# Three more groups of projections by one level of Strassen's method, with their late products moved into the next units

## The chip, the cores and the metric

One core of a Trainium2 chip runs the kernel, in float32 throughout. The metric is the device time of one execution in microseconds (us). About 0.2% is what a measurement of this kernel can tell from no change.

## What is computed

A layer of a streaming encoder on x (512 positions x 1024 channels):

```python
h = rmsnorm(x, norm_mix_g)
u, v, bg, cg, xs, ga, gb = split(h @ w_in)            # seven projections 1024 -> 1024
a = gelu(u) * (W_s[g] (block causal) rmsnorm(gelu(v)) + b_s[g])           # branch A
c = bg * causal_dwconv3(cg * xs, conv_w)                                  # branch B
m = sigmoid(ga + b) * (a @ w_proj_a) + sigmoid(gb + b) * (c @ w_proj_b)
x = x + m @ w_out
x = x + relu(rmsnorm(x, norm_ff_g) @ w_ff1)**2 @ w_ff2                    # 1024 -> 4096 -> 1024
y = rmsnorm(x, norm_final_g)
```

## The kernel before

Activations lie transposed: a tile is 128 channels by the 512 positions. Every float32 operand of TensorE is split in two, hi (a cast on ScalarE, ACT, L95) and lo (the difference, on VectorE, DVE, L96), and a product is three matmuls: hi by hi, hi by lo, lo by hi.

**A unit** is one output tile of a projection: 8 slices of the contraction x 3 = 24 matmuls of 128x512 (`unit_matmuls`, L189 to L191) with one operand of 128x1024 hi and lo. **A pair** is two output tiles of FF1 at once by one level of Strassen's method: the positions are halved, the contraction is halved, and seven products of 4 slices x 3 matmuls of 128x256 (`product`, L493 to L495; 84 matmuls) replace two units' 48. It uses combinations of the weights (three operands of 128x1024 and one of 128x512, sums on DVE in `plan_pairs`, L460, L466, L467) and of the activations (`combos`), and joins the products on DVE and ACT (`block_pair`, L514 to L529). Its seventh product P7 runs inside the next pair.

Order of the work: v, then u with the mixing of branch A behind it by LAG units (`mix`), gate A and P_A in turns, branch B (`c_units`: c, x and b of one tile in turns), gate B and P_B in turns, W_o, and four chunks of FF1 pairs and FF2 units. Only FF1 goes by pairs. A list of steps (`steps`) prepares the weights in that order: `pump` does the next step before a unit or product, when one of RING = 4 hi/lo buffers is free. A step records an ACT cast and a DVE subtraction, so both engines' queues mix the weights' work with that of the outputs. Weights come from HBM on SP's queue, 1 MB at a time into two raw buffers; the next but one is loaded when a raw buffer's last step has run. x is kept in `res` from the start to the residual of W_o. Storage is in groups by name (X, V, M, AC). The vector of per-channel constants (`vec`) comes on GpSimd's queue; the norm gain of x is a 513th column of x.

The engines' queues are in program order as the tile framework's scheduler set them.

Of the kernel before, what the change touches and what calls it, by code (L numbers as in the profile page):

```python
# [17 lines left out]
KT = D // P  # L18
NB = S // P
HALF = 512  # L20
# [6 lines left out]
RING = 4  # L27


V_BGATE, V_GV, V_CONV, V_GFF, V_GFIN, V_N = 0, 16, 24, 48, 56, 64  # L30
# [3 lines left out]
def hybrid_block(ctx, tc, xT, vecs, w_v, w_main, w_ff1, w_s, b_s, out_a, out_b):  # L34
# [16 lines left out]
    wsp = ctx.enter_context(tc.tile_pool(name="wsp", bufs=RING))  # L51
# [7 lines left out]
    nc.gpsimd.dma_start(vec, vecs)  # L59
# [17 lines left out]
    def shared(tag, bufs, name, dtype=F32):  # L77

        return big.tile([P, S], dtype, tag=tag, bufs=bufs, name=name)

    def wide(tag, name, dtype=F32, shape=(2, S)):

        return big.tile([P, *shape], dtype, tag=tag, bufs=4 if tag == "V" else 8, name=name)
# [18 lines left out]


# [3 lines left out]
    n_units = w_main.shape[0]  # L107
    steps = []
    opnds = []
    raw_of = {}  # L110

    def load(key):
        if key in raw_of:
            return
        r = raws.tile([P, 4, S], F32, name="raw")
        kind, i = key
        if kind == "u":
            nc.sync.dma_start(
                r.rearrange("p (u a) s -> p u (a s)", u=2), w_main[i : i + 2].rearrange("u p f -> p u f")
            )  # L120
        else:
            nc.sync.dma_start(r, w_ff1[i])
        raw_of[key] = r

    loads = []

    def load_after(key):

        n = loads.index(key) + 2
        if n < len(loads):  # L130
            load(loads[n])

    def add_operand(src, n=2, last=None):

        o = {"done": False, "ready": False, "idx": len(opnds)}

        def step():
            hi = wsp.tile([P, n, S], F32R, name="whi", padded_shape=[P, 2, S])
            lo = wsp.tile([P, n, S], F32R, name="wlo", padded_shape=[P, 2, S])
            split_into(hi, lo, src())  # L140
            o["hi"], o["lo"], o["ready"] = hi, lo, True
            if last:
                load_after(last)

        opnds.append(o)
        steps.append((step, o))
        return o

    def pump(n=1):

        while steps and n:
            step, o = steps[0]
            if o is not None and o["idx"] >= RING and not opnds[o["idx"] - RING]["done"]:
                return
            steps.pop(0)
            step()
            n -= 1
# [5 lines left out]
    units = []  # L163

    def plan_units(n):
        for _ in range(n // 2):
            i = len(units)
            key = ("u", i)
            loads.append(key)
            for e in range(2):  # L170
                units.append(add_operand(
                    lambda key=key, e=e: raw_of[key][:, 2 * e : 2 * e + 2, :], last=key if e else None
                ))
# [3 lines left out]
    def unit_matmuls(psum, act_hi, act_lo, start=True, stop=True, cols=slice(0, S), ks=range(KT), o=None):  # L177

        if o is None:
            o = units[state["next"]]  # L180
            state["next"] += 1
            pump()
            need(o)
            o["done"] = True
        hi, lo = (o[h].rearrange("p a s -> p (a s)") for h in ("hi", "lo"))
        for k in ks:
            c = slice(k * P, (k + 1) * P)
            first, end = start and k == 0, stop and k == KT - 1
            nc.tensor.matmul(psum, hi[:, c], act_hi[k][:, cols], start=first, stop=False)  # L189
            nc.tensor.matmul(psum, hi[:, c], act_lo[k][:, cols], start=False, stop=False)  # L190
            nc.tensor.matmul(psum, lo[:, c], act_hi[k][:, cols], start=False, stop=end)  # L191

    def bank():
        return ps.tile([P, S], F32, name="bank")
# [28 lines left out]


    resg = [big.tile([P, S + 1], F32, name=f"res{k}") for k in range(KT)]
    res = [t[:, :S] for t in resg]

    def halves_of(tag, name, dtype=F32R, n=KT):

        ts = [wide(tag, f"{name}{k}", dtype) for k in range(n)]  # L230
        return [t[:, 0, :] for t in ts], [t[:, 1, :] for t in ts]

    xh, xl = halves_of("X", "x")
    acc = shared("acc", 1, "acc")
    vtt = halves_of("V", "vt", F32, NB)
    vt = [[vtt[h][b] for h in range(2)] for b in range(NB)]
    wsT = wide("M", "wsT", F32, (KT, P))
    bsb = wide("M", "bsb", F32, (KT, P))
    vsum = small.tile([P, 2, NB], F32, name="vsum")

    vparts = {}
    vraw = []
    n_plain = n_units - NCH * KT
    plan_units(n_plain)

    def prep_v(i):
# [4 lines left out]
        if h == 0:  # L251
            nc.sync.dma_start(resg[k], xT[k])
        if i % 2 == 0:
            vraw.append(wide("AC", f"vraw{i}"))
        t = vraw[-1][:, i % 2, :]
        nc.sync.dma_start(t, w_v[h, k])
        if i == 2 * KT - 1:
            for key in loads[:2]:
                load(key)
        vp = wide("M", f"vp{h}{k}", F32R)  # L260
        vh, vl = vp[:, 0, :], vp[:, 1, :]
        if h == 0:
            split_into(xh[k], xl[k], res[k], scale=resg[k][:, S : S + 1])
        split_into(vh, vl, t)
        if h == 0:
            sum_squares(acc, res[k], k)
        vparts[i] = (vh, vl)

    def sum_squares(acc, src, k, n=S):
        if k == 0:  # L270
            nc.scalar.activation(acc, src, AF.Square)
        else:
            sq = temp("sq", n)
            nc.scalar.activation(sq, src, AF.Square)
            nc.vector.tensor_add(acc, acc, sq)
# [11 lines left out]
    V_AHEAD = 3  # L287
# [4 lines left out]
    for i in range(2 * KT):  # L292
# [6 lines left out]
        vh, vl = vparts.pop(i)  # L299
        for ws, xs in ((vh, xh), (vl, xh), (vh, xl)):  # L300
            for b in range(NB):
# [3 lines left out]
                )  # L305
        if i == KT - 1:
# [16 lines left out]
    nc.vector.tensor_copy(R, Rp)
    R2 = shared("R2", 1, "R2")
# [11 lines left out]
    ah, al = halves_of("AC", "a")  # L336
    us = {}

    def u_unit(j):
# [4 lines left out]
        u = temp("u")  # L344
        nc.scalar.activation(u, t, AF.Gelu)
        us[j] = u

    def mix(g):
# [11 lines left out]
        a = temp("a")  # L360
        nc.vector.tensor_mul(a, t, us.pop(g))
        split_into(ah[g], al[g], a)

    def c_units(j):
        pc = bank()
        unit_matmuls(pc, xh, xl)
        t = temp("t_c")
        nc.vector.tensor_mul(t, pc, R2)
        px = bank()
        unit_matmuls(px, xh, xl)  # L370
        z = temp("z", S + 2)
        nc.vector.memset(z[:, 0:2], 0.0)
        nc.vector.tensor_mul(z[:, 2 : S + 2], t, px)
        y = temp("y")
        w = [col(V_CONV + 8 * i, j) for i in range(3)]
        nc.vector.tensor_scalar(y, z[:, 0:S], w[0], None, op0=ALU.mult)
        for i in (1, 2):
            nc.vector.scalar_tensor_tensor(y, z[:, i : S + i], w[i], y, op0=ALU.mult, op1=ALU.add)
        pb = bank()
        unit_matmuls(pb, xh, xl)  # L380
        yr = temp("yr")
        nc.vector.tensor_mul(yr, y, R)
        c = temp("c")
        nc.vector.tensor_mul(c, pb, yr)
        split_into(ch[j], cl[j], c)

    def gate(n, j):
        pg = bank()
        unit_matmuls(pg, xh, xl)
        t = temp("t_g")  # L390
        nc.vector.tensor_mul(t, pg, R)
        sg = temp("sig")
        nc.scalar.activation(sg, t, AF.Sigmoid, bias=col(V_BGATE + 8 * n, j))
        return sg

    LAG = 2
    for j in range(KT):
        u_unit(j)
        if j >= LAG:
            mix(j - LAG)  # L400


    m1p = halves_of("V", "m1", F32, KT // 2)
    m1 = [m1p[k % 2][k // 2] for k in range(KT)]
    for j in range(KT):
        sg = gate(0, j)
        if j == 0:
            for g in range(KT - LAG, KT):
                mix(g)
        pp = bank()  # L410
        unit_matmuls(pp, ah, al)
        nc.vector.tensor_mul(m1[j], pp, sg)


    ch, cl = halves_of("AC", "c")
    for j in range(KT):
        c_units(j)

    mh, ml = halves_of("M", "m")
    for j in range(KT):  # L420
        sg = gate(1, j)
        pp = bank()
        unit_matmuls(pp, ch, cl)
        m = temp("m")
        nc.vector.tensor_mul(m, pp, sg)
        nc.vector.tensor_add(m, m1[j], m)
        split_into(mh[j], ml[j], m)

    N2 = S // 2
    KS = KT // 2

    cmb = [wide("X", f"cmb{i}", F32R) for i in range(8)] + [wide("V", f"cmv{i}", F32R) for i in range(4)]
    b11 = [wide("AC", f"b11{i}", F32R) for i in range(2)]
    sums_t = [wide("AC", f"wsum{i}") for i in range(4)]
    right = {}
    for sl in range(KS):
        for hl in range(2):  # L440
# [322 lines left out]
```

## Time and profile before

| what | value |
|---|---|
| median of 3 runs | 802.61 us (802.58 to 803.2) |
| the profiled execution | 802.63 us |
| its span, first to last instruction | 800.7 us (1.9 us lie around it) |
| PE, DVE, ACT busy | 792.6, 485.4, 293.6 us |
| mean granted TensorE clock | 0.998 |

Busy time is the sum of an engine's instruction spans, overlaps counted once. A PE start-to-start distance is the pace at which matmuls follow each other; one matmul's own span (0.39 or 0.28 us) overlaps with the next.

### The profile page before, as it was taken

The page shows a single profiled execution, that of the slowest core. Times are in us where ns is not written, and L with a number is a line of the kernel's source. Part 1 is how long each engine was busy: PE and PEld are TensorE (multiplying, and loading weights), DVE is VectorE, ACT ScalarE, POOL GpSimd, SP SyncE. Part 2 cuts the span into 40 slices and gives each one's busy share as a digit, 9 for nine tenths or more (in the row PEclk, how much of TensorE's full clock was granted, in tenths as well). Part 3 has the DMA queues.
Part 4 walks back from the last instruction along what each step waited for, and adds up shares of the span by engine and source line. Part 5 has one row for each costly group of instructions (what it writes and reads, how often), then busy time and mean ns, then how long its engine had stood idle before and what let it go on. Part 6 is the DMA issues. An engine that isn't in the chain of part 4 may idle for free.

```text
span 800.7 us, 10145 instructions
## 1 busy us (share of the span) xinstructions
PE 792.6 (99%) x4222; PEld 684.2 (85%) x4222; DVE 485.4 (61%) x702; ACT 293.6 (37%) x420; POOL 7.6 (1%) x15
## 2 busy tenths in 40 slices
PE   9999999999999999999999999999999999999996
PEld 6888888888888888888888899889988999889886
DVE  7645663333654555454458999655975598457744
ACT  8423342222222222233245656413651265225521
POOL 0000000000000000000000100000000000000000
PEclk9999999999999999999999999999999999999999
DMA  9512132223323223332222123422332224313303
GB/s 329 203 49 105 53 105 88 74 102 106 106 105 97 69 97 107 106 106 92 71 100 105 57 103 106 158 86 72 106 106 105 90 73 156 105 53 106 106 1 106
DMA packets 22221, 81.42 MB, mean 102 GB/s; under 512 B 1680, under 2 KB 2704, under 8 KB 20128
## 3 DMA queue, kind: packets, MB, share of 16 engines
q1 hardware_dynamic: 21280, 79.18, 28.6%
q10 hardware_dynamic: 864, 1.57, 0.5%
q8 instruction: 33, 0.54, 0.3%
q14 instruction: 12, 0.10, 0.0%
q0 software_dynamic: 32, 0.03, 0.0%
HBM read 78.68 MB, written 2.10 MB: 101 GB/s over the span
## 4 chain that ended last, share of the span: by engine, by line
PE 98%; DVE 1%; DMA 0%; ACT 0%; POOLq 0%; DVEq 0%; issue 0%
PE bank L190 24%; PE bank L189 24%; PE bank L191 24%; PE bank L493 7%; PE bank L494 7%; PE bank L495 6%; PE bank L302 5%; PE bank L351 1%; DMA res<-xT 0%; PE bank L221 0%; DVE wlo L96 0%; PE bank L600 0%; DVE cmv L96 0%; PE st L646 0%; PE st L210 0%; DVE ob L612 0%
## 5 line engine op out<-in xcount | busy, mean ns | idle before, releaser
L95 ACT CAST whi<-raw 128x1024 fp32r<-128x1024 f32 (+1 forms) x136 | 135.2, 1003 | 347.0 <-PE bank L190 305.4
L96 DVE TENSOR_TENSOR wlo<-raw,whi 128x1024 fp32r<-128x1024 f32 (+1 forms) x136 | 157.5, 1159 | 13.6 <-ACT whi L95 13.0
L189 PE MATMUL bank<-x,whi 128*128 128x512 f32 x384 | 150.0, 391 | 0.0
L190 PE MATMUL bank<-x,whi 128*128 128x512 f32 x384 | 149.4, 389 | 0.0
L191 PE MATMUL bank<-x,wlo 128*128 128x512 f32 x384 | 149.4, 389 | 0.0
L191 PEld LDWEIGHTS bank<-x,wlo 128*128 128x128 f32 x384 | 72.1, 188 | 14.9
L190 PEld LDWEIGHTS bank<-x,whi 128*128 128x128 f32 x384 | 72.1, 188 | 14.8
L189 PEld LDWEIGHTS bank<-x,whi 128*128 128x128 f32 x384 | 72.1, 188 | 14.8
L189 PE MATMUL bank<-zm,whi 128*128 128x512 f32 (+1 forms) x204 | 77.0, 378 | 0.0
L191 PE MATMUL bank<-zm,wlo 128*128 128x512 f32 (+1 forms) x204 | 76.9, 377 | 0.0
L190 PE MATMUL bank<-zm,whi 128*128 128x512 f32 (+1 forms) x204 | 76.8, 377 | 0.0
L493 PE MATMUL bank<-cmb,whi 128*128 128x256 f32 x256 | 73.1, 286 | 0.0
L495 PE MATMUL bank<-cmb,wlo 128*128 128x256 f32 x256 | 72.4, 283 | 0.0
L494 PE MATMUL bank<-cmb,whi 128*128 128x256 f32 x256 | 72.4, 283 | 0.0
L690 DVE TENSOR_TENSOR res<-bank,res 128x512 f32<-128x512 f32 x30 | 20.8, 692 | 69.6 <-PE bank L191 69.6
L95 ACT CAST whi<-wsum 128x1024 fp32r<-128x1024 f32 x32 | 33.6, 1049 | 67.1 <-PE bank L494 35.9
L493 PEld LDWEIGHTS bank<-cmb,whi 128*128 128x128 f32 x256 | 49.1, 192 | 1.3 <-ACT c L520 1.0
L494 PEld LDWEIGHTS bank<-cmb,whi 128*128 128x128 f32 x256 | 49.1, 192 | 0.0
L495 PEld LDWEIGHTS bank<-cmb,wlo 128*128 128x128 f32 x256 | 49.1, 192 | 0.0
L96 DVE TENSOR_TENSOR wlo<-wsum,whi 128x1024 fp32r<-128x1024 f32 x32 | 39.2, 1224 | 15.2 <-ACT whi L95 14.6
L190 PEld LDWEIGHTS bank<-zm,whi 128*128 128x128 f32 x204 | 38.4, 188 | 7.0
L191 PEld LDWEIGHTS bank<-zm,wlo 128*128 128x128 f32 x204 | 38.4, 188 | 7.0
(158 smaller groups left out, 1328.6 us busy)
## 6 DMA issues: line engine op xcount, KB each, us to landing
raw<-w_main SPq DMA_DIRECT2D x52, 1024.0 KB, 4.9
raw<-w_ff SPq DMA_DIRECT2D x16, 1024.0 KB, 4.7
vraw<-w_v SPq DMA_DIRECT2D x16, 256.0 KB, 5.4
res<-xT SPq DMA_DIRECT2D x8, 256.5 KB, 5.4
out_a<-o SPq DMA_DIRECT2D x4, 256.0 KB, 2.3
wsT<-w_sT ACTq DMA_DIRECT2D x2, 256.0 KB, 5.6
bsb<-b_sb ACTq DMA_DIRECT2D x2, 256.0 KB, 4.2
out_b<-ob ACTq DMA_DIRECT2D x2, 256.0 KB, 3.0
```

The lines of the kernel that those rows point to most:

```text
L95: nc.scalar.copy(hi, src)
L96: nc.vector.tensor_tensor(lo, src, hi.bitcast(F32), op=ALU.subtract)
L189: nc.tensor.matmul(psum, hi[:, c], act_hi[k][:, cols], start=first, stop=False)
L190: nc.tensor.matmul(psum, hi[:, c], act_lo[k][:, cols], start=False, stop=False)
L191: nc.tensor.matmul(psum, lo[:, c], act_hi[k][:, cols], start=False, stop=end)
L302: nc.tensor.matmul(vbanks[h][b], xs[k][:, b * P : (b + 1) * P], ws, start=k == 0 and ws is vh and xs is xh, stop=k == KT - 1 and xs is xl,)
L351: nc.tensor.matmul(pm[:, b * P : (b + 1) * P], vt[b][g // 4][:, (g % 4) * P : (g % 4 + 1) * P], wsT[:, g, :], start=True, stop=True,)
L493: nc.tensor.matmul(out, w_hi, x_hi, start=first and sl == 0, stop=False, skip_group_check=True)
L494: nc.tensor.matmul(out, w_hi, x_lo, start=False, stop=False, skip_group_check=True)
L495: nc.tensor.matmul(out, w_lo, x_hi, start=False, stop=sl == KS - 1, skip_group_check=True)
L690: nc.vector.tensor_add(res[j], py, res[j])
```

## The change

The gates (16 units become 8 pairs) and the streams c and x of branch B (16 units become 8 pairs) go by pairs as FF1 does; u, v, b, P_A, P_B, W_o and FF2 stay units. The combinations of the activations for these pairs are made once, in the v and u stages (`x_combos`, four times). A pair has two PSUM banks instead of three, in the order P1, P2, E, P6, F; its last two products, P7 and D, are put on a list, and `run_late` runs one in the middle of the next unit and one behind it, or two places inside a next pair. That holds for FF1 too. The second output of a pair comes out negated, in two halves, and the code behind it takes that in. x is not kept but loaded again (8 x 256 KB) ahead of W_o; `vec` comes on ACT's queue and holds the norm gain; storage is 32 slots that are taken and given back first in, first out; LAG is 3.

```diff
-    nc.gpsimd.dma_start(vec, vecs)
+    nc.scalar.dma_start(vec, vecs)
...
-            split_into(xh[k], xl[k], res[k], scale=resg[k][:, S : S + 1])
+            split_into(xh[k], xl[k], xin[k], scale=col(V_GMIX, k))
...
+        tl["a1"] = add_operand(lambda: raw(0, 2))
+        add_step(add1)
+        tl["s31"] = add_operand(lambda: s31)
+        add_step(add2)
+        tl["s42"] = add_operand(lambda: s42)
+        tl["a22"] = add_operand(lambda: raw(2, 3), n=1)
+        add_step(lambda: load(ld + 2))
...
+        for k in range(KT):
+            if k == 0 or k == KT // 2:
+                pump()
+                need(o)
+            unit_k(psum, o, k, act_hi, act_lo)
+            if k == KT // 2 - 1:
+                run_late()
+        release(o)
+        run_late()
...
+        ba, be = bank(), bank()
+        A, P2, E = ba[:, :N2], ba[:, N2:], be[:, :N2]
+        c1, c2 = temp("c1"), temp("c2")
+        product(p, right, "P1", A, True)
+        product(p, right, "P2", P2, False)
+        nc.scalar.copy(c1[:, :N2], A)
+        nc.vector.tensor_add(c1[:, :N2], P2, c1[:, :N2])
+        run_late()
+        product(p, right, "E", E, True)
+        product(p, right, "P6", A, False)
+        nc.scalar.copy(c2[:, N2:], E)
+        run_late()
+        product(p, right, "F", E, False)
+        nc.scalar.copy(c1[:, N2:], A)
+        nc.vector.tensor_add(c1[:, N2:], E, c1[:, N2:])
+        first(c1)
+
+        def p7():
+            product(p, right, "P7", A, False)
+            nc.scalar.copy(c2[:, :N2], A)
+            nc.vector.tensor_add(c2[:, N2:], c2[:, :N2], c2[:, N2:])
+
+        def dd():
+            product(p, right, "D", A, False)
+            second(A, c2)
+
+        late.extend([p7, dd])
...
-    LAG = 2
+    LAG = 3
...
+        block_pair(next_pair(), right_x, c_first, c_second)
+        block_pair(next_pair(), right_x, x_first, x_second)
+        pbs = []
+        for e in range(2):
+            pbs.append(bank())
+            unit_matmuls(pbs[e], xh, xl)
+        for e in range(2):
+            nc.vector.tensor_mul(ys[e], pbs[e], ys[e])
+            split_into(ch[j0 + e], cl[j0 + e], ys[e])
...
+    for k in (0, 4, 1, 5, 2, 6, 3, 7):
+        nc.sync.dma_start(res[k], xT[k])
```

`first` of a gate multiplies by R and takes the sigmoid (two instructions, L560, L561), `second` the same in two halves (L565, L566, then L567); `x_first` and `x_second` multiply c by x and run the convolution (L618, L620 twice, L621).

**Place 1, DVE, branch B.** One tile of branch B before: c's product with R squared (L368), c by x (L373), the convolution (L376, L378), and b (L384), between weights' lo parts (L96).

```order
L368 TENSOR_TENSOR t_c_1674<-bank_1643,R2_516 128x512 [waits PE_49]
L372 MEMSET z_1705 128x2
L96 TENSOR_TENSOR wlo_1678<-raw_1575,whi_1677 128x1024 [waits DMAHW5_49,Activation_49]
L373 TENSOR_TENSOR z_1705<-t_c_1674,bank_1676 128x512 [waits DVE_49,PE_49]
L376 TENSOR_SCALAR y_1708<-z_1705,vec_79 128x512 [waits DVE_49]
L96 TENSOR_TENSOR wlo_1714<-raw_1575,whi_1713 128x1024 [waits Activation_49]
```

After the change, the end of a round of two tiles and the start of the next one (L118 is the lo part, L218 the first weight sum, L645 the product with b, L301 the first join of the next c pair).

```order
L620 SCALAR_TENSOR_TENSOR y_2596<-z_2592,vec_76,y_2596 128x512 [waits DVE_49]
L118 TENSOR_TENSOR wlo_2656<-wsum1_104,whi_2655 128x1024 [waits Activation_49]
L621 TENSOR_TENSOR y_2596<-y_2596,R_537 128x512 [waits DVE_49]
L218 TENSOR_TENSOR wsum0_103<-raw_2562 128x1024 [waits DMAHW3_49]
L645 TENSOR_TENSOR y_2596<-bank_2601,y_2596 128x512 [waits DVE_49,PE_49]
L118 TENSOR_TENSOR wlo_2705<-raw_2562,whi_2704 128x1024 [waits Activation_49]
L118 TENSOR_TENSOR c5_1690<-y_2596,c5_1690 128x512 [waits Activation_49]
L301 TENSOR_TENSOR c1_2639<-bank_2637,c1_2639 128x256 [waits Activation_49]
```

A round of two tiles has 42 DVE instructions in the second list; in the first, one tile has 12. The join L301 now stands behind the convolution and four weight steps of the round before.

**Place 2, PE, gate A.** Before, unit follows unit, and a wait stands only where a unit takes a new operand.

```order
L190 MATMUL bank_1035<-x7_121,whi_941 128x512
L191 MATMUL bank_1035<-x7_121,wlo_942 128x512
L189 MATMUL bank_1070<-a0_533,whi_971 128x512 [waits Activation_49]
L190 MATMUL bank_1070<-a0_533,whi_971 128x512
L191 MATMUL bank_1070<-a0_533,wlo_972 128x512 [waits DVE_49]
L189 MATMUL bank_1070<-a1_534,whi_971 128x512
```

After, in a gate pair: E (x by xc13) ends, three matmuls of a P_A unit and the first of F (x4, x5) are put in, and P6 (xc20, into bank_1317, which held P1) waits for DVE's join L301.

```order
L284 MATMUL bank_1318<-xc13_646,whi_1249 128x256
L285 MATMUL bank_1318<-xc13_646,wlo_1250 128x256
L265 MATMUL bank_1401<-a0_732,whi_1335 128x512 [waits Activation_49]
L266 MATMUL bank_1401<-a0_732,whi_1335 128x512
L267 MATMUL bank_1401<-a0_732,wlo_1336 128x512 [waits DVE_49]
L283 MATMUL bank_1318<-x4_113,whi_1283 128x256 [waits Activation_49]
L284 MATMUL bank_1318<-x4_113,whi_1283 128x256
L285 MATMUL bank_1318<-x4_113,wlo_1284 128x256
L283 MATMUL bank_1318<-x5_114,whi_1283 128x256
L284 MATMUL bank_1318<-x5_114,whi_1283 128x256
L283 MATMUL bank_1317<-xc20_442,whi_1283 128x256 [waits DVE_49]
L284 MATMUL bank_1317<-xc20_442,whi_1283 128x256
```

A wait for DVE now stands in the middle of the pair, on a bank and not on a weight.

## Rows read from the trace of the kernel before

**Rows 1.** The page: busy time, share and instructions of each engine.

```profile
PE 792.6 (99%) x4222; PEld 684.2 (85%) x4222; DVE 485.4 (61%) x702; ACT 293.6 (37%) x420; POOL 7.6 (1%) x15
```

**Rows 2.** The page: the chain that ended last, shares by engine.

```profile
PE 98%; DVE 1%; DMA 0%; ACT 0%; POOLq 0%; DVEq 0%; issue 0%
```

**Rows 3.** Timeline of PE in branch B: start us, us, engine, line, operation.

```profile
214.67 0.39 PE L189 MATMUL bank<-x,whi 128*128 128x512 f32 x1
...
216.71 0.39 PE L189 MATMUL bank<-x,whi 128*128 128x512 f32 x1
```

**Rows 4.** Timeline of PE in an FF1 pair.

```profile
569.80 0.28 PE L493 MATMUL bank<-cmb,whi 128*128 128x256 f32 x1
...
571.12 0.28 PE L495 MATMUL bank<-cmv,wlo 128*128 128x256 f32 x1
```

**Rows 5.** Windows, branch B and FF1: length; PE, PEld, DVE, ACT, POOL busy (x); clock, DMA, GB/s.

```profile
195.00:325.00 130.00, 130.00 (x575) 107.67 (x574) 70.36 (x96) 28.87 (x33) 0.00 (x0) 1.00 0.29 96
553.00:583.00 30.00, 30.00 (x253) 30.00 (x251) 25.59 (x40) 18.82 (x31) 0.00 (x0) 1.00 0.32 106
```

**Rows 6.** Groups of DVE by form: busy us, mean ns of one | idle before.

```profile
L96 DVE TENSOR_TENSOR wlo<-raw,whi 128x1024 fp32r<-128x1024 f32 x120 | 146.7, 1222 | 13.6 <-ACT whi L95 13.0
L378 DVE SCALAR_TENSOR_TENSOR y<-z,vec,y 128x512 f32<-128x512 f32 x16 | 12.0, 749 | 0.3
L96 DVE TENSOR_TENSOR wlo<-raw,whi 128x512 fp32r<-128x512 f32 x16 | 10.9, 683 | 0.0
L521 DVE TENSOR_TENSOR c<-bank,c 128x256 f32<-128x256 f32 x16 | 6.7, 419 | 0.2
```

**Rows 7.** Timeline of DVE in FF1, where neighbours are independent.

```profile
565.78 1.22 DVE L96 TENSOR_TENSOR wlo<-wsum,whi 128x1024 fp32r<-128x1024 f32 x1
566.91 0.68 DVE L96 TENSOR_TENSOR z<-c,z 128x512 fp32r<-128x512 f32 x1
567.52 0.42 DVE L521 TENSOR_TENSOR c<-bank,c 128x256 f32<-128x256 f32 x1
567.85 0.68 DVE L466 TENSOR_TENSOR wsum<-wsum,raw 128x512 f32<-128x512 f32 x1
```

**Rows 8.** Timeline of DVE in branch B, where the second uses the first's output.

```profile
199.91 0.69 DVE L373 TENSOR_TENSOR z<-t_c,bank 128x512 f32<-128x512 f32 x1 [3.31 <-PE bank L191]
200.63 0.49 DVE L376 TENSOR_SCALAR y<-z,vec 128x512 f32<-128x512 f32 x1
```

**Rows 9.** Timeline of PE at a chunk's end, where a product waited for ACT's copy.

```profile
585.87 0.40 PE L190 MATMUL bank<-zm,whi 128*128 128x512 f32 x1
586.17 0.39 PE L493 MATMUL bank<-cmb,whi 128*128 128x256 f32 x1
586.40 0.28 PE L494 MATMUL bank<-cmb,whi 128*128 128x256 f32 x1
586.51 0.28 PE L495 MATMUL bank<-cmb,wlo 128*128 128x256 f32 x1
```

**Rows 10.** Timeline of ACT there: the copy stood behind a cast.

```profile
500.18 1.05 ACT L95 CAST whi<-raw 128x1024 fp32r<-128x1024 f32 x1 [1.38 <-PE bank L494]
501.13 0.36 ACT L520 COPY c<-bank 128x256 f32<-128x256 f32 x1
```

**Rows 11.** The chain at gate A's start, in order of time: two mixes.

```profile
105.39 1.78 PE bank L351 x16
```

**Rows 12.** The chain at the kernel's start, in order of time.

```profile
0.74 2.72 DMA res<-xT
3.46 0.02 issue
3.49 0.72 ACT x L98
```

**Rows 13.** DMA issues: count, KB each, median us from issue to landing.

```profile
raw<-w_main SPq DMA_DIRECT2D x52, 1024.0 KB, 4.9
res<-xT SPq DMA_DIRECT2D x8, 256.5 KB, 5.4
vec<-vecs POOLq DMA_DIRECT2D x1, 32.0 KB, 3.5
```

More of the change, by code (lines that the diff above doesn't have):

```diff
@@ L101, in split_into, with bank, load @@
             )
-    n_units = w_main.shape[0]
+    def bank():
+        return ps.tile([P, S], F32, name="bank")
     steps = []
-    opnds = []
     raw_of = {}
-    def load(key):
-        if key in raw_of:
+    loads = []
+    wfree = list(range(N_WBUF))
+    a22_busy = [False]
+    def load(n):
+        if n >= len(loads) or n in raw_of:
             return
+        kind, i = loads[n]
         r = raws.tile([P, 4, S], F32, name="raw")
-        kind, i = key
         if kind == "u":
@@ L163, in hybrid_block @@
     units = []
+    pairs = []
     def plan_units(n):
         for _ in range(n // 2):
-            i = len(units)
-            key = ("u", i)
-            loads.append(key)
+            ld = len(loads)
+            loads.append(("u", len(units)))
             for e in range(2):
-                units.append(add_operand(
-                    lambda key=key, e=e: raw_of[key][:, 2 * e : 2 * e + 2, :], last=key if e else None
-                ))
-    state = {"next": 0}
[L177 to L184, printed above, removed]
-        hi, lo = (o[h].rearrange("p a s -> p (a s)") for h in ("hi", "lo"))
[L186 to L191, printed above, removed]
@@ new lines, in hybrid_block, with run_late, flush_late, unit_matmuls @@
+    late = []
+    def run_late():
+        if late:
+            late.pop(0)()
+    def flush_late():
+        while late:
+            run_late()
+    state = {"next": 0}
+    def unit_matmuls(psum, act_hi, act_lo):
+        o = units[state["next"]]
+        state["next"] += 1
+        for k in range(KT):
[7 more added lines that the diff above has]
+        run_late()
@@ new lines, in product @@
+    def product(p, right, name, out, first):
+        t, g, r = LEFT[name]
+        o = pairs[p][t]
+        pump()
+        need(o)
+        for sl in range(KS):
+            c = slice(sl * P, (sl + 1) * P)
+            w_hi, w_lo = o["hi"][:, g, c], o["lo"][:, g, c]
+            x_hi, x_lo = right[r, sl, 0], right[r, sl, 1]
+            nc.tensor.matmul(out, w_hi, x_hi, start=first and sl == 0, stop=False, skip_group_check=True)
+            nc.tensor.matmul(out, w_hi, x_lo, start=False, stop=False, skip_group_check=True)
+            nc.tensor.matmul(out, w_lo, x_hi, start=False, stop=sl == KS - 1, skip_group_check=True)
+        if name in ("P2", "D", "F", "P7"):
+            release(o)
@@ L222, in spread @@
         return pt
[L225 to L246, printed above, removed]
-        if i >= 2 * KT:
-            pump()
-            return
-        h, k = divmod(i, KT)
[L251 to L262, printed above, removed]
-            split_into(xh[k], xl[k], res[k], scale=resg[k][:, S : S + 1])
[L264 to L267, printed above, removed]
     def sum_squares(acc, src, k, n=S):
@@ L275, in sum_squares, with prep_v @@
             nc.vector.tensor_add(acc, acc, sq)
+    sums_t = slots(2, "wsum")
+    plan_units(KT)
+    for _ in range(KS):
+        plan_pair()
+        plan_units(2)
+    for _ in range(KS):
+        plan_pair()
+        plan_pair()
+        plan_units(2)
+    for _ in range(KS):
+        plan_pair()
+        plan_units(2)
+    plan_units(KT)
+    n_win = len(pairs)
+    for ck in range(NCH):
+        for _ in range(CF // 2 + (ck == 0) - (ck == NCH - 1)):
+            plan_pair()
+        plan_units(KT)
+    xin_s = slots(KS, "xin")
+    xin = halves(xin_s)
+    x_s = slots(KT, "x", F32R)
+    xh, xl = hi_lo(x_s)
+    acc = small.tile([P, S], F32, name="acc")
+    vt_s = slots(NB, "vt")
+    vt = [[s.t[:, h, :] for h in range(2)] for s in vt_s]
+    vp_s, vraw_s = [], []
+    ws_s = None
+    vsum = small.tile([P, 2, NB], F32, name="vsum")
+    vparts = {}
+    V_AHEAD = 3
+    V_RAW = 3
+    def prep_v(i):
+        if i >= 2 * KT:
+            pump()
+            return
+        h, k = divmod(i, KT)
+        if h == 0:
+            nc.sync.dma_start(xin[k], xT[k])
+        if i % 2 == 0:
+            if len(vraw_s) >= V_RAW:
+                vraw_s.pop(0).give()
+            vraw_s.append(Slot(f"vraw{i}"))
+        t = vraw_s[-1].t[:, i % 2, :]
+        nc.sync.dma_start(t, w_v[h, k])
+        if i == KT + 1 or i == KT + 4:
+            load(0 if i == KT + 1 else 1)
+        vp = Slot(f"vp{h}{k}", F32R)
+        vh, vl = vp.t[:, 0, :], vp.t[:, 1, :]
+        if h == 0:
+            split_into(xh[k], xl[k], xin[k], scale=col(V_GMIX, k))
+        split_into(vh, vl, t)
+        if h == 0:
+            sum_squares(acc, xin[k], k)
+        vparts[i] = vp
     def v_gelu(h, b):
@@ L399, in hybrid_block, with gate, first, second @@
         if j >= LAG:
             mix(j - LAG)
[L403 to L407, printed above, removed]
+    right_x = right_of(
+        lambda sl, hl: x_s[sl].t[:, hl, :N2], x_s[KS:], xc1, xc2
+    )
+    def gate(p, n, j0, then):
+        def first(c1):
+            nc.vector.tensor_mul(c1, c1, R)
+            nc.scalar.activation(c1, c1, AF.Sigmoid, bias=col(V_BGATE + 8 * n, j0))
+            then(j0, c1)
+        def second(n21, c2):
+            nc.vector.tensor_mul(c2[:, :N2], n21, R[:, :N2])
+            nc.vector.tensor_mul(c2[:, N2:], c2[:, N2:], R[:, N2:])
+            nc.scalar.activation(c2, c2, AF.Sigmoid, bias=col(V_BGATE + 8 * n, j0 + 1), scale=-1.0)
+            then(j0 + 1, c2)
+        block_pair(p, right_x, first, second)
@@ L408, in hybrid_block, with next_pair @@
+    pair_no = {"next": 0}
+    def next_pair():
+        pair_no["next"] += 1
+        return pair_no["next"] - 1
+    m1_s = []
+    sgs = {}
+    for p in range(KS):
+        gate(next_pair(), 0, 2 * p, sgs.__setitem__)
+        if p == 0:
             for g in range(KT - LAG, KT):
                 mix(g)
[L410 to L419, printed above, removed]
@@ new lines, in hybrid_block, with split_m @@
+    for p in range(KS):
+        c_pair(2 * p)
+    m_s = []
+    done_m = [0]
+    def split_m(upto):
+        for j in range(done_m[0], upto):
+            m_s.append(Slot(f"m{j}", F32R))
+            split_into(m_s[j].t[:, 0, :], m_s[j].t[:, 1, :], m1[j])
+        done_m[0] = upto
+    for p in range(KS):
+        gate(next_pair(), 1, 2 * p, sgs.__setitem__)
+        last = p == KS - 1
+        for e in range(2):
+            j = 2 * p + e
+            pp = bank()
+            unit_matmuls(pp, ch, cl)
+            if last and e == 0:
+                give(*x_s, *xc1, *xc2)
+                split_m(j)
+            nc.vector.tensor_mul(sgs[j], pp, sgs[j])
+            nc.vector.tensor_add(m1[j], m1[j], sgs.pop(j))
+            if last:
+                split_m(j + 1)
```

437 lines of the change are left out of this document (221 added, 216 removed).

## The prediction

> **What bounds the kernel now.** I read the busy shares first: PE is busy 99% of the span, DVE 61%, ACT 37% [rows 1]. The chain that ended last says the same: 98% of it is PE [rows 2]. So time is what the matmuls take at their pace, and an edit counts in two ways only: by matmul time removed, and by new places where PE waits. The timeline of PE gives the pace. Ten 512-column matmuls in a row start over 216.71 - 214.67 = 2.04 us, 0.2267 us apart [rows 3]; twelve of 256 columns over 1.32 us, 0.120 apart [rows 4]. The granted clock is 1.00, the higher level of 2.4 GHz, in both stretches [rows 5], so nothing is to be had there. The windows show what other engines have to spare: in branch B DVE is busy 70 of 130 us, in FF1, where all goes by pairs, 25.6 of 30 [rows 5]; there PE still keeps its pace. The new stages will look like the second of these, and that is the question.
>
> **The matmuls removed.** Two units are 48 x 0.2267 = 10.88 us, a pair is 84 x 0.120 = 10.08: 0.80 less. Seven products instead of eight would be an eighth of 10.88, 1.36; the 36 more matmuls take back the rest, since one of half the columns takes more than half the time. Sixteen pairs are new (4 gate A, 8 for c and x, 4 gate B): **-12.8 us**, all on the path.
>
> By the Trainium skill, "TensorE: Matmul & The Clock Gate", section on the back-to-back issue gap, a matmul of N columns takes N/2.4 + 2.5 ns, so 216 and 109 ns; by that the term would be 16 x (48 x 0.2158 - 84 x 0.1092) = 19.0 us and the total 787.7. The trace shows 227 and 120, so it does not agree, and the rows decide.
>
> **The start.** x's split (L98 before) now also waits for `vec`, which holds the gain. x landed at 3.46 and the split began at 3.49 [rows 12]; `vec` took 3.5 us from issue to landing on GpSimd's queue [rows 13]. On ACT's queue no row shows it. If it is as slow from an issue at 0.74, it lands at 4.24, 0.75 late; if it is as quick as x, nothing is lost. Neither end is nearer, so I take the middle: **+0.4**.
>
> **The first gate pair.** LAG 3 puts three mixes instead of two behind it; two took 1.78 us [rows 11], and the work only moves. But the last mixes' results now come out while DVE also joins the pair. After the pair's F, PE does the mixes (2.4 us, by that row), half a P_A unit (2.7) and P7 (1.4), then the unit's slices 4 to 7; it wants the lo part of a7 some 8.8 us after F. DVE has by then two joins and scalings, three L356-like instructions (0.75 each, as [rows 6] for that kind), three multiplications, a 1.22 us weight part and three lo parts in its queue: about 9.2 with hops. Before the pair, the join that P6 waits for stands behind some 5.5 us of DVE work against 5.3 of PE's. Together **+0.7**; bounds 0, if starts overlap as in [rows 7], and 2.
>
> **The other seven gate pairs.** P6 writes the bank whose first half the join L301 must have read: the wait in Place 2. P6 comes 5.6 us into the pair (36 matmuls of P1, P2, E, then five of F, at 0.12, and three of 0.2267). In DVE's queue L301 stands behind the multiplication of the tile before, a lo part, a weight sum of 128x1024 and one of 128x512 and another lo part. By starts (1.13 for 1024 columns, 0.61 for 512, 0.33 for 256 [rows 7]) that chain ends 5.1 us in; by full durations (1.22, 0.68, 0.42 [rows 6]) at 5.7. Where PE found an input late, it lost 0.07 at the waiting matmul and 0.11 at the next (0.30 and 0.23 us where 0.227 and 0.12 are the pace [rows 9]). I take **+0.25** each, **+1.75**; bounds 0 and 3.
>
> **The four rounds of branch B.** A round is two pairs and two units: 31.04 us of PE. DVE has 42 instructions in it: ten 1024 columns wide, fourteen of 512, four like L378, two like L376, ten of 256, two tiny. By durations [rows 6, 8] that is 30.1 us, by starts 26.8. More sharply, there is a loop. P6 of c starts 4.9 us into a round (41 matmuls), F of x ends at 17.3 (144 matmuls): 12.4 of PE. From that F to the join L301 of the next round, which its P6 awaits, DVE has 28 instructions (the end of this run is Place 1): six of 1024, ten of 512, four like L378, two like L376, five of 256. By starts, with 0.08 more for each of five that use the output of their neighbour and so do not overlap [rows 8], it takes 18.5 us; by durations 20.3. With 0.4 for the two hand-overs the loop is 31.3 or 33.1. The neighbours in the list are mostly independent, which is the case of [rows 7], so I take 31.3: **+0.3** a round, **+1.2**; the other end is +2.0 a round, +8.
>
> By the Trainium skill, "VectorE: DVE Perf Modes", section Terms, the pipeline is flushed after each DVE operation and the next is not issued until it is empty. By that the durations add up, and the rounds cost 8 us. The trace has starts 0.08 ahead of the previous end, so it shows an overlap, if a small one; hence a rival, below.
>
> **What costs nothing, and its cover.** The combinations of x: four times some 3.0 us of DVE (four of 256, two of 512 columns) in stages where DVE has time; its idle 39% is the cover, and without it 3 us each would show. FF1: per pair DVE does 11.1 us instead of 11.8 (of 256 columns five instructions either way, of 512 one less), and P7 and D come later, with an output only FF2 awaits; I take 0, bounds -1.2 (the waits at the chunks' ends go) and +1.5 (they come inside pairs). The reload of x, 8 x 256 KB: such a transfer took 5.4 us [rows 13], W_o's first output comes some 20 us behind the issue; the weights queued behind it on SP are fetched two loads, some 20 us, ahead, and a load takes 4.9 [rows 13]. The weights' bytes are unchanged. Moving `vec` frees GpSimd, which nobody waits for.
>
> **The sum**, against the profiled execution's 802.63 us (the median, 802.61, is the same): 802.63 - 12.8 + 0.4 + 0.7 + 1.75 + 1.2 = **793.9 us**.
>
> **Rivals.**
> *DVE paces branch B.* For it: 30.1 us of durations in 31.0. Against it: [rows 7], and FF1, where 25.6 of 30 costs PE nothing. At 33 us a round the time is 793.9 - 1.2 + 8 = 800.7; half of it, if only the dependent half adds up, 797.
>
> *No stall at all*, the scheduler having put each wait behind enough matmuls: 802.63 - 12.8 = 789.8, or 788.6 with FF1's small gain.
>
> *Hand-overs at every pair: slower.* F writes over E, which ACT must have copied (L305) within P6's 1.44 us. An ACT copy can stand behind a cast of 1.05 and take 0.36 [rows 10]; with a hop of 0.2 it ends 1.6 after E. F is then 0.2 late and pays 0.18 for the restart [rows 9]; P7 and D wait for ACT too. At 0.45 us for each of all 32 pairs, FF1's included, since they have the new order too, this is 14.4: 802.63 - 12.8 + 0.4 + 14.4 = 804.6. It decides from 0.39 a pair. Against it: ACT is busy only 18.8 of 30 us where pairs are dense [rows 5], the copies of a gate pair stand one behind another with no cast between, and one copy late by 0.2 in a few pairs is already in my terms.
>
> *The change doesn't do what it says*: in PE's order the 84 short matmuls stand where 48 long ones stood, so I give this nothing.
>
> **How the numbers follow.** What can be told from no change is 0.2%, 801.0 to 804.2. Chances: the forecast, 790 to 796.5, 0.70; no stall, below 790, 0.08; DVE pacing the rounds in part or whole, 796.5 to 801.5, 0.14, of which 0.03 above 801.0; a mixture of that with hand-overs, 801 to 804.2, 0.03; hand-overs at every pair, above 804.2, 0.05. So faster 0.70 + 0.08 + 0.11 = 0.89, same 0.06, slower 0.05. The range that holds 8 in 10 starts at the case without stalls, 789.8, and ends at 800.0, inside the DVE case.
>
> **What would show it.** The pace: pairs in gate A at 0.120 a matmul and 10.1 us each. The start: x's split held by `vec`'s transfer by some 0.4 us. The waits: P6 behind DVE's L301, 0.2 to 0.3 us each, four times in branch B and up to eight in the gates. A round of branch B at 31.3 us with DVE busy some 28 of it. PE's busy share again near 99%. I am wrong if rounds last 32.5 us or more with DVE without a gap (DVE paces), if the chain of waits shows ACT's copies L305 or L308 ahead of F and P7 in most pairs (hand-overs), or if 256-column matmuls come slower than 0.120 with operands that lie elsewhere.

## The result and the profile after

The change takes 795.81 us (median of four executions, 794.87 to 796.82) against 802.73 before on the same chip: a ratio of 0.9913, with a 95% interval of 0.9896 to 0.9930. Forecast was 793.9, in a range of 789.8 to 800.0. The profiled execution is the slowest of the four, 796.82 us with a span of 795.0.

The page of the changed kernel has, in its parts 1 and 4 (compare [rows 1, 2]):

```profile
PE 786.3 (99%) x4798; PEld 703.6 (88%) x4798; DVE 567.1 (71%) x854; ACT 362.6 (46%) x548; POOL 6.3 (1%) x14
...
PE 90%; DVE 4%; DMA 3%; ACT 1%; issue 1%; POOLq 0%; DVEq 0%; ACTq 0%
```

PE is as busy as before, but the chain of what ended last now leaves it: 10% of it lies outside PE, most of that on DVE, DMA and ACT, against 2% before. That does not mean that 10% was lost. Where a product waits even 0.2 us, the chain goes back through the whole queue of the engine that it waited for.

Where each stage begins is read from the timeline of PE, at the first matmul of a stage. Of the kernel before, branch B, gate B, W_o and FF1 begin here:

```profile
188.83 0.39 PE L189 MATMUL bank<-x,whi 128*128 128x512 f32 x1
...
319.39 0.39 PE L189 MATMUL bank<-x,whi 128*128 128x512 f32 x1
...
406.43 0.39 PE L189 MATMUL bank<-m,whi 128*128 128x512 f32 x1
...
449.95 0.28 PE L493 MATMUL bank<-b,whi 128*128 128x256 f32 x1
```

And of the change:

```profile
187.21 0.28 PE L283 MATMUL bank<-x,whi 128*128 128x256 f32 x1
...
312.25 0.28 PE L283 MATMUL bank<-x,whi 128*128 128x256 f32 x1
...
397.04 0.39 PE L265 MATMUL bank<-m,whi 128*128 128x512 f32 x1
...
440.56 0.28 PE L283 MATMUL bank<-fb,whi 128*128 128x256 f32 x1
```

With u at 50.71 and 51.54, gate A at 99.69 and 99.61, and the last transposes at 791.36 and 785.84, the stages' lengths are:

| stage | before, us | after, us | difference | forecast |
|---|---|---|---|---|
| start and v | 50.71 | 51.54 | +0.83 | +0.4 |
| u with mixes, gate A (a mix moves from one to the other) | 138.12 | 135.67 | -2.45 | -3.2 + 0.7 + 0.75 |
| branch B | 130.56 | 125.04 | -5.52 | -6.4 + 1.2 |
| gate B | 87.04 | 84.79 | -2.25 | -3.2 + 1.0 |
| W_o | 43.52 | 43.52 | 0 | 0 |
| FF1 and FF2 to the transposes | 341.41 | 345.28 | **+3.87** | 0 |
| transposes to the end | 9.3 | 9.2 | -0.2 | 0 |

The stages that were changed by intent gave 10.2 us, 1.1 more than forecast. FF1, which was to cost nothing, gave 3.9 of it back. These are lengths in the slowest of the four executions.

**The gates' waits.** The timelines of DVE and PE in the second gate pair, which began at 123.51:

```profile
127.61 1.22 DVE L118 TENSOR_TENSOR wlo<-raw,whi 128x1024 fp32r<-128x1024 f32 x1
128.75 0.42 DVE L301 TENSOR_TENSOR c<-bank,c 128x256 f32<-128x256 f32 x1
```

```profile
129.02 0.28 PE L284 MATMUL bank<-x,whi 128*128 128x256 f32 x1
129.22 0.39 PE L283 MATMUL bank<-xc,whi 128*128 128x256 f32 x1
129.44 0.28 PE L284 MATMUL bank<-xc,whi 128*128 128x256 f32 x1
```

The join ended 5.66 us into the pair (forecast 5.1 to 5.7), P6 started at 5.71, and PE lost 0.08 before it and 0.10 behind it. (A matmul's loss is what its distance to the next start has above the pace.)

**Branch B.** The end of DVE's list of a round, and P6 of the next one, which began at 249.99:

```profile
253.63 0.69 DVE L118 TENSOR_TENSOR c<-y,c 128x512 fp32r<-128x512 f32 x1
254.23 0.42 DVE L301 TENSOR_TENSOR c<-bank,c 128x256 f32<-128x256 f32 x1
```

```profile
254.90 0.28 PE L283 MATMUL bank<-xc,whi 128*128 128x256 f32 x1
255.02 0.28 PE L284 MATMUL bank<-xc,whi 128*128 128x256 f32 x1
```

The join ended at 254.65, 0.25 us before P6: no wait. Rounds two to four take 31.13 us each, (312.25 - 218.86) / 3, with 31.04 of matmul time.

**FF1.** At the end of its first pair the norm's short matmuls (L359) stand behind F in PE's queue. The timeline:

```profile
444.64 0.38 PE L283 MATMUL bank<-ft,whi 128*128 128x256 f32 x1
444.64 0.69 DVE L379 TENSOR_TENSOR acc<-acc,sq 128x512 f32<-128x512 f32 x1
...
445.38 1.05 PE L359 MATMUL st<-inv_d,acc 128*128 128x1 f32 x8 [0.36 <-DVE acc L379]
```

The windows there (columns as in [rows 5]):

```profile
445.00:447.00 2.00, 1.50 (x12) 1.27 (x11) 2.00 (x5) 1.78 (x4) 0.00 (x0) 1.00 0.00 0
447.00:449.00 2.00, 2.00 (x10) 2.00 (x11) 2.00 (x3) 0.18 (x1) 0.79 (x1) 0.51 0.04 8
449.00:451.00 2.00, 2.00 (x13) 2.00 (x13) 1.10 (x5) 0.37 (x1) 1.12 (x1) 0.64 0.00 0
```

PE waited for the sum of squares, and behind that its granted clock was at the lower level, 1.2 GHz, for some 3.5 us: 16 matmuls at 0.21 us instead of 0.12. In the pairs behind it PE waited again and again for a join or a copy. Here P6, the second of these matmuls, begins 0.20 us late, behind L301, and pays 0.10 more at its next step:

```profile
478.32 0.28 PE L284 MATMUL bank<-ft,whi 128*128 128x256 f32 x1
478.64 0.39 PE L283 MATMUL bank<-ft,whi 128*128 128x256 f32 x1
478.87 0.28 PE L284 MATMUL bank<-ft,whi 128*128 128x256 f32 x1
```

At the end of FF1 the chain has a lo part of z that FF2 needs, behind a weight's lo part (the load of these weights had landed only at 741.0). The chain, and PE's timeline there:

```profile
743.26 1.22 DVE wlo L118
744.48 0.61 DVE z L118
745.09 0.04 issue
745.14 0.50 PE bank L266
```

```profile
744.27 0.50 PE L265 MATMUL bank<-z,whi 128*128 128x512 f32 x1
745.14 0.50 PE L266 MATMUL bank<-z,whi 128*128 128x512 f32 x1 [0.36 <-DVE z L118]
```

PE's starts split the 3.9 us by place. Above the pace, FF1's start (up to the spread of the norm) lost 2.8 us, 0.9 before; the pairs behind it 2.5, 1.1 before; the lo part of z 0.7, 0.2 before: 1.9 + 1.4 + 0.6. Of the 1.9, some 1.5 is the low clock.

### The profile page after: what moved, and what is told of

Read it like the earlier page. It is cut to its first block, busy times and chain, and to the rows that moved or that the text cites. A ratio compares the mean times of both kernels' runs of the same rounds, so it can differ in the third digit from the quotient of the medians.

```text
span 795.0 us, 11578 instructions
## 1 busy us (share of the span) xinstructions
PE 786.3 (99%) x4798; PEld 703.6 (88%) x4798; DVE 567.1 (71%) x854; ACT 362.6 (46%) x548; POOL 6.3 (1%) x14
## 4 chain that ended last, share of the span: by engine, by line
PE 90%; DVE 4%; DMA 3%; ACT 1%; issue 1%; POOLq 0%; DVEq 0%; ACTq 0%
PE bank L266 16%; PE bank L265 16%; PE bank L267 16%; PE bank L283 12%; PE bank L285 11%; PE bank L284 11%; PE bank L476 6%; DVE wlo L118 2%; DMA raw<-w_pair 1%; DMA raw<-w_main 1%; ACT whi L117 1%; PE bank L530 1%; DMA vec<-vecs 0%; DVE z L118 0%; DVE wsum L218 0%
## 5 line engine op out<-in xcount | busy, mean ns | idle before, releaser
L118 DVE TENSOR_TENSOR wlo<-raw,whi 128x1024 fp32r<-128x1024 f32 (+1 forms) x136 | 148.6, 1095 | 16.7 <-ACT whi L117 14.9
L266 PE MATMUL bank<-z,whi 128*128 128x512 f32 (+1 forms) x272 | 102.7, 377 | 0.4 <-DVE z L118 0.4
L265 PE MATMUL bank<-z,whi 128*128 128x512 f32 (+1 forms) x272 | 102.8, 378 | 0.0
L267 PE MATMUL bank<-z,wlo 128*128 128x512 f32 (+1 forms) x272 | 102.4, 377 | 0.0
L118 DVE TENSOR_TENSOR wlo<-wsum,whi 128x1024 fp32r<-128x1024 f32 x64 | 78.2, 1221 | 26.6 <-ACT whi L117 26.2
L283 PE MATMUL bank<-ft,whi 128*128 128x256 f32 x256 | 73.7, 288 | 0.2
L283 PE MATMUL bank<-xc,whi 128*128 128x256 f32 x256 | 73.2, 286 | 0.2
L284 PE MATMUL bank<-ft,whi 128*128 128x256 f32 x256 | 73.0, 285 | 0.0
L285 PE MATMUL bank<-ft,wlo 128*128 128x256 f32 x256 | 72.5, 285 | 0.0
L285 PE MATMUL bank<-xc,wlo 128*128 128x256 f32 x256 | 72.4, 283 | 0.0
L284 PE MATMUL bank<-xc,whi 128*128 128x256 f32 x256 | 72.4, 283 | 0.0
L266 PEld LDWEIGHTS bank<-z,whi 128*128 128x128 f32 x272 | 51.2, 188 | 9.7 <-DVE z L118 0.7
L265 PEld LDWEIGHTS bank<-z,whi 128*128 128x128 f32 x272 | 51.2, 188 | 9.3 <-ACT z L117 0.3
L283 PE MATMUL bank<-fb,whi 128*128 128x256 f32 x192 | 54.9, 286 | 0.0
L283 PE MATMUL bank<-x,whi 128*128 128x256 f32 x192 | 54.5, 284 | 0.0
L284 PE MATMUL bank<-fb,whi 128*128 128x256 f32 x192 | 54.4, 284 | 0.0
L285 PE MATMUL bank<-fb,wlo 128*128 128x256 f32 x192 | 54.3, 284 | 0.0
L284 PE MATMUL bank<-x,whi 128*128 128x256 f32 x192 | 54.3, 283 | 0.0
```

The costliest lines, as they stand in the source:

```text
L118: nc.vector.tensor_tensor(lo, src, hi.bitcast(F32), op=ALU.subtract)
L265: nc.tensor.matmul(psum, hi[:, c], act_hi[k][:, cols], start=k == 0, stop=False)
L283: nc.tensor.matmul(out, w_hi, x_hi, start=first and sl == 0, stop=False, skip_group_check=True)
L284: nc.tensor.matmul(out, w_hi, x_lo, start=False, stop=False, skip_group_check=True)
L285: nc.tensor.matmul(out, w_lo, x_hi, start=False, stop=sl == KS - 1, skip_group_check=True)
```

## The experiments

My theory after the result: the new pairs do what was forecast, and FF1 lost 3.9 us by its own new order of the pair. Rivals: the low clock is the whole of it; the single set of weight sums; the stages hold each other up.

**1. The norm's matmuls behind the next pair's P7.**

```diff
-            r2 = rstd_of(acc)
-            nc.vector.tensor_copy(Rf, spread(r2))
-            wait_rf.pop()()
+            p7 = late[0]
+            def p7_then_norm():
+                p7()
+                r2 = rstd_of(acc)
+                nc.vector.tensor_copy(Rf, spread(r2))
+                wait_rf.pop()()
+            late[0] = p7_then_norm
```

> Theory: in the changed kernel the short matmuls of the norm stand in PE's queue right behind F of the first FF1 pair and wait 0.6 us for the sum of squares, and the low clock behind that pause (granted 0.51 to 0.64 for some 3.6 us in the profiled execution, about 1.6 us lost) comes from it. With the norm moved behind the next pair's P7 PE does not pause there: 792.3 to 794.5 us in all executions, granted clock 1.00 at FF1's start. Rival 1: the low clock has nothing to do with the pause; then the executions fall in two groups as before, near 793 and 795, and a window of low clock is there in some. Rival 2: the late norm holds up the first outputs of FF1; then 796 or more.

795.15 us (794.79 to 796.3), ratio 0.9907 (0.9890 to 0.9924). The clock stayed at 1.00 in the profile, and FF1 and FF2 took 343.9 us. But PE now waited 0.8 us elsewhere, where the norm is spread over the tile. In the stage that is 1.4 us of the loss, not the whole; the medians (795.15 and 795.81) are not apart by more than the noise. The forecast of 794.5 at most fell.

**2. FF1's pairs as before; the rest as in the change.**

```diff
+    def plan_ff_pair(i):
...
+        def sm(e):
+            return (sums_2 if i % 2 else sums_t)[e].t
...
+        tl["a1"] = add_operand(lambda: raw(0, 2))
+        add_step(add1)
+        tl["a22"] = add_operand(lambda: raw(2, 3), n=1)
+        add_step(add2)
+        tl["s42"] = add_operand(lambda: sm(1))
+        tl["s31"] = add_operand(lambda: sm(0))
...
-        block_pair(n_win + p, right_f, first, second)
+        ff_pair(n_win + p, right_f, after)
```

`ff_pair` is the old `block_pair`: P1, P2, then the late P7 of the pair before, D, F, P6, E, in three banks. The old handling of the outputs, both behind P7, comes back with it.

> FF1's pairs as in the kernel before (three banks, D early, only P7 late, two pairs of weight sums); gates and branch B by pairs as in the change. Theory: the stage from the first FF1 pair on, 3.7 us longer in the change's profile than before, is longer because of the new order of FF1's pairs (joins L301 that P6 waits for, the norm's wait, the last lo part of z), so it comes back to 350.5 to 351.5 us, and the total is 792 to 793.5. Rival: the loss is of something else (the single set of slots, the weights' new order, which stay): 795 to 797, the stage at 353 or more.

792.83 us (792.14 to 793.15), ratio 0.9874 (0.9859 to 0.9888). The first FF1 matmul and the first transpose, from the timeline:

```profile
439.57 0.28 PE L311 MATMUL bank<-fb,whi 128*128 128x256 f32 x1
...
781.16 0.93 PE L807 MATMUL bank<-ident,res 128*128 128x128 f32 x7
```

341.6 us: the loss is gone, with the single store of slots and the reloaded x still there. The theory held. No run separates the order from the third bank and from the handling of the outputs.

**3. c and x as units again.** `c_units` of the kernel before, and its 24 units in the plan, in place of `c_pair` and eight pairs.

> Branch B's c and x as units again, the gates by pairs. Theory: the terms add up by stage; branch B took 130.6 us before and 125.0 with the change, so this is 5.5 slower than the change: 800.3 to 802.3, branch B at 130.5, the other stages as in the change. Rival: the rounds' DVE work also slows what stands around them (the first gate pairs behind, the weights' loads); then the total is below 800.

800.15 us (799.57 to 801.17), ratio 0.9967 (0.9955 to 0.9978). Branch B took 130.56 us again, from 187.63 to 318.19, 5.5 more than in the change; FF1 and FF2 took 343.9, 1.4 less than in the change: the wait for the lo part of z (0.7) was not there, and the pairs waited some 0.6 less. So the stage's term adds up, but FF1 was not "as in the change". The median lies 0.15 us below the expected band; the profiled execution (801.17) lies in it.

**4. P7 and D at once in gates and branch B.**

```diff
-        late.extend([p7, dd])
+        if p < n_win:
+            p7()
+            dd()
+        else:
+            late.extend([p7, dd])
```

> P7 and D of the gates' and branch B's 16 pairs directly behind F instead of inside the next units or pair; FF1 unchanged. Theory: D must wait for ACT's copy of the sum behind P7 (a hop of 0.2, the copy 0.36, 0.18 for the restart), some 0.7 us in each of 16 pairs: 804 to 809, and the chain of waits shows D behind L314. Rival: the scheduler fills the wait with matmuls of the unit behind, as it did at P6: 795 to 798.

798.5 us (797.86 to 799.55), ratio 0.9947 (0.9932 to 0.9962). From the waits (in total us, times, longest):

```profile
PEld bank L283 <- ACT c L314: 4.8, 16, 0.4
PEld bank L283 <- ACT c L305: 2.6, 13, 0.2
```

The wait is where the theory put it, once in each of the 16 pairs, but 0.30 and not 0.7 us: the scheduler moved matmuls of the unit behind into the gap (four of P_A's between P7 and D of the second gate pair, from 133.09). Both expectations missed. By the medians the late products are worth 2.7 us here, 0.17 a pair. By the stages it is more: W_o began at 400.71 instead of 397.04, 3.7 later, and FF1 and FF2 were 1.4 shorter, as in run 3.

**5. The changed kernel again.**

> The changed kernel itself, beside the three others: 794.8 to 796.9 us, in two groups. Where the granted clock falls at FF1's start, the execution should belong to the upper group if the clock is what parts them.

796.0 us (795.42 to 796.62). The two with a mean granted clock of 0.996 took 796.45 and 796.62, the two with 0.997 took 795.54 and 795.42. That is as expected; the last section has an execution that does not fit.

**6. The last sum of squares ahead of the combinations.**

```diff
+        if n == KT - 1:
+            sum_squares(acc, res[j], n)
         if n % 2:
             split_into(fb2[j - KS].t[:, 0, :], fb2[j - KS].t[:, 1, :], xg[j])
```

(and not behind them for that tile)

> Of W_o's last tile the sum of squares is taken ahead of the combinations for FF1 instead of behind them. Theory: the norm's short matmuls then wait less than 0.2 us instead of 0.6 behind the first pair, PE does not pause, and if the pause is what the low clock follows, the clock stays at 1.00: 793.2 to 794.6 us. Rival: the combinations come 1.3 us later for it, and the first pair's E or P6 waits instead, with the clock as low behind that pause: 795 to 797.

795.63 us (794.76 to 796.78), ratio 0.9913 (0.9898 to 0.9927): no gain. The windows of PE (length, PE busy, clock, DMA share, GB/s) show that the wait only moved, to the spread of the norm, which waits 1.8 us for DVE, and that the clock stayed up this time:

```profile
444.00:446.00 2.00, 0.76 (x7) 1.00 0.00 0
446.00:448.00 2.00, 1.47 (x12) 1.00 0.04 8
448.00:450.00 2.00, 2.00 (x17) 1.00 0.00 0
```

Of its four executions the two with a mean clock of 0.998 took 794.76 and 795.21, the two with 0.995 took 796.05 and 796.78.

**7. More work for DVE in branch B.**

```diff
             nc.vector.tensor_mul(y, y, R)
+            for _ in range(2):
+                nc.vector.tensor_mul(acc, y, R)
+                nc.vector.tensor_mul(acc, y, R2)
             ys[e] = y
```

> Eight more DVE instructions of 128x512 in each round of branch B (products into a tile that nobody reads). Theory: DVE is the next limit there. By starts (0.61 us each) a round's DVE work is 26.9 + 4.9 = 31.8 us, more where they use each other's output, and the loop from x's F to the next join L301 is up to 4.9 longer against a margin of 0.25: rounds of 32 to 34.5 us instead of 31.13, 799 to 809 in all, DVE without a gap in the rounds. If durations added up (30.1 + 5.5), 35.6 or more a round, 814. Rival: DVE has room that the list does not show: 795 to 797.

800.61 us (799.3 to 803.87), ratio 0.9976 (0.9965 to 0.9988). A window of the change from its second round, and then two of this run from its third and fourth:

```profile
219.00:250.00 31.00, 31.00 (x218) 29.06 (x217) 27.35 (x43) 13.14 (x21) 0.00 (x0) 1.00 0.30 101
```

```profile
250.00:281.00 31.00, 30.57 (x212) 28.26 (x211) 29.92 (x48) 12.55 (x19) 0.00 (x0) 1.00 0.29 103
281.00:312.00 31.00, 29.35 (x206) 27.22 (x205) 30.21 (x48) 12.88 (x20) 0.00 (x0) 1.00 0.30 103
```

DVE is now busy 97% of the time and PE is not. Rounds two to four run from 218.21 to 315.86, 32.55 us each, for 50 DVE instructions. By durations these are 30.1 + 5.5 = 35.6 us. So DVE takes its instructions at the distance of their starts, as in [rows 7], and it was the next limit, by my estimate some 3.5 us a round away: eight starts of 0.61 us are 4.9, and 1.42 of them showed. The queue's order changed with the edit: the longest waits of PE in these rounds are for a weight's lo part (1.0 us), and none of those that the view of waits lists is for the join L301.

**8. The second run's kernel with squares first, and F ahead of D in the first FF1 pair.**

```diff
+        if p == n_win:
+            product(p, right, "F", F, True, ())
+            product(p, right, "D", Dp, True, fr)
+        else:
+            product(p, right, "D", Dp, True, fr)
+            product(p, right, "F", F, True, fr)
```

> FF1's pairs as in the kernel before, gates and branch B as in the change, and at FF1's start two things more: the sum of squares ahead of the last combinations, and F ahead of D in the first pair alone. Theory: of the 1.4 us that the second run still loses around FF1's start (PE waits of 0.24, 0.43 and 0.25 us and what follows them) at least half goes: 791.3 to 792.2 us. Rival: the waits only move to the late combinations: 792.5 to 793.2.

792.99 us (792.63 to 793.26), ratio 0.9879 (0.9863 to 0.9896): the same as run 2. PE's waits moved to the norm's spread (0.45 us), as in run 1.

**9 and 10. One or two sets of weight sums.** Run 9 is the change with two sets in turns in FF1; run 10 is run 2 with one. The edit of run 10 against run 2:

```diff
-            return (sums_2 if i % 2 else sums_t)[e].t
+            return sums_t[e].t
```

> The change with one thing of the old FF1: two sets of weight sums in turns instead of one; the new order of the pair stays. Theory (the order costs): FF1's joins still stand late in DVE's queue, and the norm still waits right behind F: 794.7 to 796.7 us, the stage from the first FF1 pair to the last transposes at 344 to 345.5. Rival (the single set costs, since a pair's first sum must wait for the lo part of the sum before it): 792.3 to 793.5, stage 342 or less.

799.44 us (799.14 to 801.01), ratio 0.9962 (0.9949 to 0.9976), worse than the change and than run 2. The second set let a weight's sum and lo part come ahead of FF1's last combinations in DVE's queue. The chain, with the columns of [rows 12]:

```profile
445.16 0.42 DVE T2T L346
445.58 1.17 DVE wlo L118
446.75 0.61 DVE ft L118
447.36 0.04 issue
447.41 0.58 PE bank L289
```

PE lost 1.7 and 1.2 us at two waits there, and ran at the lower clock behind them. The theory's number missed on the other side, but the single set is not the cause.

> The second run's kernel (FF1's pairs in the old order, three banks, only P7 late) with one set of weight sums instead of two. Theory (the order costs): 792.1 to 793.4 us, the stage at 341.3 to 342.2. Rival (the single set costs): 794.5 to 796.5, stage 344 or more.

**792.03 us (791.6 to 792.77), ratio 0.9865 (0.9852 to 0.9879)**, FF1 and FF2 in 340.8 us:

```profile
439.54 0.28 PE L311 MATMUL bank<-fb,whi 128*128 128x256 f32 x1
...
780.31 0.93 PE L806 MATMUL bank<-ident,res 128*128 128x128 f32 x7
```

The waits of PE's weight loads (PEld) for another engine's join or copy, in the change and then here:

```profile
PEld bank L283 <- DVE c L301: 2.8, 10, 0.6
...
PEld bank L283 <- ACT c L305: 1.4, 7, 0.2
```

```profile
PEld bank L311 <- ACT c L366: 1.3, 4, 0.3
...
PEld bank L311 <- DVE c L329: 0.9, 3, 0.3
...
PEld bank L311 <- ACT c L333: 0.8, 4, 0.2
```

(L366 is FF1's copy behind P6, which P7 waits for; L329 and L333 are the join and the copy of E in gates and branch B, L301 and L305 above.) Gates and branch B by pairs with late products, FF1 by pairs in the old order, one set of sums: this has the lowest time of the study. It beats the kernel before and the change; its interval overlaps that of run 2, so one set of sums is not shown to be better than two here.

## Why the prediction was right, and where it was not

**The matmuls removed, -12.8.** Right. The pace is 0.120 in the new pairs (254.90 to 255.02), and branch B as units (run 3) is 5.5 us longer. The Trainium skill gives N/2.4 + 2.5 ns in "TensorE: Matmul & The Clock Gate" (Back-to-back issue gap), for an isolated matmul as that section says; the estimate of 109 ns from it did not hold in these rows of a dense stream.

**The gates, +2.45 in all.** Measured 1.7: u, gate A and gate B gave 4.7 of 6.4 us. The waits were P6 behind L301, in the place forecast: about 0.2 in each later pair of gate A, and 0.39, 0.17, 0.10 and nothing in gate B. The 0.39 stood behind a weight sum for which DVE itself waited 0.32 us, for the weights' load. The first gate pair's 0.7 did not come: PE lost 0.1 in it, and had no wait for the lo part of a7. (The forecast put three mixes at 2.4 us by [rows 11], where two at 1.78 make 2.7.)

**Branch B, +0.3 a round.** The loop was forecast at 31.3 and measured at no more than 31.13, since the join came 0.25 us ahead of P6; DVE took 18.5 us from the end of x's F (the next matmul starts at 236.16) to the join's end (254.65), the number forecast. Only the first round waited, 0.6. Run 7 shows the rival's mechanism where it really starts, and that durations don't add up: successive starts lie 0.60 us apart (253.63 to 254.23) where one instruction lasts 0.69. In the Trainium skill, "VectorE: DVE Perf Modes" (Terms), the next operation cannot issue until the pipeline is empty; the prediction took this to mean that durations add up, and that reading does not fit these rows.

**The start, +0.4.** `vec` landed 3.02 us after its issue and x's split began at 3.77 instead of 3.49. The u stage began 0.2 to 0.4 us later than before in the profiles of runs 2, 5, 6, 7, 9 and 10, and 0.7 to 1.3 later in those of the change and of runs 1, 3, 4 and 8, with more waits in v; why these come and go wasn't tried.

**FF1, "I take 0, bounds -1.2 and +1.5".** This is the step that failed: +3.87 in the profile, beyond its bound. I counted DVE's work per pair (less) and P7 and D coming later (harmless), and did not ask what is now *close behind* DVE's results. Three things were: the norm behind F of the first pair, now one product earlier than before (0.6 us, and some 1.5 of low clock in part of the executions); P6 and F a product behind the join or copy they wait for where no late product stands between (0.16 to 0.32 us at each chunk's start and in a few pairs, 1.4 more in all than before); and the last lo part of z (0.64). Run 2 takes all of it back, and runs 9 and 10 exclude the weight sums. Runs 1, 6 and 8 each moved a wait, and another took its place. The low clock's 1.5 belongs to executions like the profiled one; run 1's profile, at a clock of 1.00 throughout FF1's start, still has 2.5 us more in FF1 and FF2 than before.

**The rival "hand-overs at every pair"** fell for the changed kernel: ten waits for L301 and seven for L305 in 32 pairs, 4.2 us in all, not 14. It was right about the place, P7, D and F behind ACT's copies: that is where run 4 lost its 2.7.

**The total.** The profiled execution lies 2.9 us above the forecast, the median 1.9. That is less than FF1's 3.9, because the changed stages came out 1.1 us better than forecast. That the two errors have opposite signs is luck.

## What to carry to other kernels

When a change is applied to code that already had the method, cost that code's new order as carefully as the new use: here, in the profiled execution, the old use lost over a third of what the new uses gained. The price of an instruction in DVE's busy queue was the distance of starts, and the margin of a wait is read where a join ends ahead of the matmul that waits for it: 0.25 us was enough for no loss at all. Where several results of one engine are all just in time, moving one wait only shows the next; change the order that brought them so close.

## What was not expected of the hardware

The granted clock fell to its lower level, 1.2 GHz, for some 3.5 us at FF1's start in the profiles of the change (twice) and of runs 3, 4 and 7, behind waits of PE around its short matmuls, and cost about 1.5 us. In run 9 it fell behind the longer waits of the first pair, for over 6 us. It did not in those of runs 1, 2, 8 and 10, and not in that of run 6, where PE was busy only 0.76 of 2 us there; yet two other executions of run 6 had a mean clock of 0.995 and took 1.4 us longer. So a pause doesn't settle it, and what does stays open. Nor does it explain every spread: one execution of the change took 796.71 us at a mean clock of 0.998.
